# A hybrid decoder trunk (gated linear recurrence beside stick-breaking attention): one f32 copy of the mixer's output, and one split per engine and level of the recurrence

## The chip, the cores and the metric

The kernel runs on one core of a Trainium2 chip. The metric is the device time of one execution in microseconds (us). A core has five engines that work from their own instruction queues: PE (TensorE, matrix multiplies), DVE (VectorE), ACT (ScalarE), POOL (GpSimd) and SP, which here issues nearly all DMAs. An instruction starts when all ahead of it in its own queue have started and what it waits for in the others is done.

## The reference

One layer, 2048 rows, width 1024. The normalised rows are projected to 4096 columns; four heads A (a gated linear recurrence, 128 wide) and eight heads B (stick-breaking attention, 64 wide) each give 512 columns; both go through a normalisation and a gate, then one output projection. A per-layer embedding is projected, normalised, gated and added; a last normalisation ends it.

```
u = rmsnorm(h, norm_g);  proj = u @ w_in
k_a = (1 - lb) * sigmoid(-a_f);  f = 1 - k_a;  q_a = silu(a_q)
S_t = diag(f_t) S_{t-1} + k_t v_t^T;   o_t = S_t^T q_t              # group A
A[t,s] = sigmoid(z_ts) * prod_{s<j<t} (1 - sigmoid(z_tj)), s < t    # group B
y = concat(headnorm(o_a) * silu(a_g), headnorm(o_b) * silu(b_g))
h = h + y @ w_out
pe = rmsnorm(p @ w_ple_proj);  gate = sigmoid(rmsnorm(h) @ w_ple_gate)
out = rmsnorm(h + gate * pe)
```

## The kernel before, in words

Every large product is made from float16 parts: a float32 operand is stored as a high and a low half (`split`, L75: an ACT copy that rounds, L76, then a DVE instruction that takes the remainder, L77), and three matmuls (high·high, high·low, low·high) make one product.

The 2048 rows are four chunks of 512 (`CH`), done last chunk first. The columns are eight groups, B0, A0, B1, A1 to B3, A3; a group is one pair of B heads or one A head. The main loop (L829 to L843) goes over 8 groups x 4 chunks = 32 units. The projection of a unit (`proj_A` L407, `proj_B` L432) is the stream of PE work; while it runs, the rest of the earlier unit (`mix_A` L483, `mix_B` L596), the preparation of the rows (`prep_x`) and of the next group's weights are stepped in between. The kernel text gives this interleaving by a count of PE work; a scheduler then sets the final order in each engine's queue from its own times, so a change in one place can move instructions elsewhere.

`mix_A` is the recurrence over one chunk as a tree of seven levels. `kq` holds k (elements 0 to 511 of a row) and q (512 to 1023) in float32. At level lv, in blocks of B = 2^lv columns, the early half of each pair of blocks of q meets the late half of k: 12 small matmuls (`lps`, 64 columns) per level, 84 per unit and 1344 in all. `parts(lv)` (L499) splits 256 elements of q into the tiles `qch`, `qcl` (packed) and, from level 1, 256 elements of k into `kp0` or `kp1` by turns, in place; the other elements of those are zero (L490, a POOL memset of 1024 elements per unit) or come from the level before. k's first split (L492) and its last (L555) have 512 elements. `update(lv)` multiplies the rest of q and k by the decay (L514). L555's result is transposed by DMA for the state's update.

```
def parts(lv):
    B = 1 << lv
    qc[lv] = f16("qch", (P, CH // 2)), f16("qcl", (P, CH // 2))
    split(q3(qc[lv][0], B), q3(qc[lv][1], B), v4(q_, B)[:, :, 0, :], p2(SQF))
    if lv > 0:
        kh, kl = kp[(lv + 1) % 2]
        split(v4(kh, B)[:, :, 1, :], v4(kl, B)[:, :, 1, :], v4(k_, B)[:, :, 1, :], p2(SKB))
```

`y_out` (L374) ends every unit: it splits the unit's 512 x 128 result y (`ys`, 512 elements per partition) and stores both halves to the DRAM tensors `y_d`. The final stage (L853 to L872) goes over 16 blocks of 128 rows: `final_out` (output projection: 48 matmuls from `fy`, 12 of the embedding), `final_tr`, `final_gate` (48 matmuls). `fy` comes from DMA transposes out of `y_d`, one chunk at a time (L695, L701, L859).

The program begins with `prep_first` (L262): rows of x (`kq_t`, `gs_t`, `e_t`) are loaded and squared on ACT (L291), the first weights are split (L132 on ACT, L133 on DVE, both scaled by `gm`, which POOL multiplies once at L277), and x is turned on PE into `xt` and split into `xh`, `xl`. `prep_x` then loads the next rows into `raw_t` and squares them (L231).

Of the kernel before, what the change touches and what calls it, by code (L numbers as in the profile page):

```python
# [28 lines left out]
def p2(e):  # L29
    return float(2.0 ** e)  # L30
# [3 lines left out]
def trunk_kernel(  # L34
# [25 lines left out]
    BUFS = dict(jk=1, kq=2, fa=2, e0=2, e1=2, gs=3, qs0=2, qs1=2, kn=1, sc=2, y=2, kp0=1, kp1=1, qh=2, ql=2, qch=2, qcl=2,  # L60
                vh=2, vl=2,  ys=1, wt=2, at=2, raw=5)
# [4 lines left out]
    def f16(tag, shape=(P, CH)):  # L66
        return wk.tile(list(shape), F16, name=tag + "_t", tag=tag, bufs=BUFS[tag])
# [44 lines left out]
    y_d = [dt_(f"y{n}_d", [S, D]) for n in "hl"]  # L112
# [261 lines left out]
    def y_out(y, eg, c):  # L374

        ys = f16("ys", (P, 2, CB, P))
        split(ys[:, 0], ys[:, 1], y, p2(SY))
        for i in range(2):
            dst = y_d[i][c * CH : (c + 1) * CH, eg * P : (eg + 1) * P]
            if (eg, c) == (LAST, NC - 1):  # L380
                if i == 0:
                    y_fetch(c)
                nc.sync.dma_start(yt[c][i][:, eg, :].rearrange("p (b t) -> p b t", t=P), ys[:, i].rearrange("p b e -> p (b e)"), transpose=True)
            nc.sync.dma_start(dst.rearrange("(b p) e -> p b e", p=P), ys[:, i])
# [22 lines left out]
    def proj_A(u, g, h, c):  # L407
        w = ws[g]
        kq, f_ = f32("kq", (P, 2, CH)), f32("fa")
        k_, q_ = kq[:, 0, :], kq[:, 1, :]  # L410

        def use(i, ps):
            if i == 0:
                nc.scalar.activation(k_, ps, AF.Sigmoid, scale=-UN)
                nc.vector.tensor_scalar(k_, k_, oml[:, h : h + 1], None, op0=ALU.mult)
                nc.vector.tensor_scalar(f_, k_, -1.0, 1.0, op0=ALU.mult, op1=ALU.add)
            else:
                nc.scalar.activation(q_, ps, AF.Sigmoid, scale=UN)
                nc.vector.scalar_tensor_tensor(q_, ps, UN, q_, op0=ALU.mult, op1=ALU.mult)
# [61 lines left out]
    state = {}  # L481

    def mix_A(h, c, kq, f_, vh, vl, gs):  # L483
# [67 lines left out]
        split(qh, ql, q_, p2(SQF))  # L551
# [129 lines left out]
    def done(eg, c):

        if eg != LAST or c in yt:
            return
        y_tiles(c)

    def y_tiles(c):
        n = NC - 1 - c
        pool, tags = ((kv, ("bkv0", "bkv1")), (xpool, ("xh0", "xl0")))[n % 2]
        if n < 2:  # L690
            yt[c] = [pool.tile([P, KD, CH], F16, name="fy", tag=t) for t in tags]
        else:
            yt[c] = yt[c + 2]

    def y_fetch(c):  # L695

        y_tiles(c)
        for ks in (slice(0, LAST), slice(LAST + 1, KD)):
            for i in range(2):
                src = y_d[i][c * CH : (c + 1) * CH, ks.start * P : ks.stop * P]  # L700
                nc.sync.dma_start(yt[c][i][:, ks, :], src, transpose=True)  # L701
# [151 lines left out]
    for c in reversed(range(NC)):  # L853
        while c not in yt:
            if not step_tasks(99):
                clock[0] = min(t.ready for t in tasks)
        yh, yl = yt[c]
        for i in range(2 if c < NC - 1 else 0):
            nc.sync.dma_start(yt[c][i], y_d[i][c * CH : (c + 1) * CH, :], transpose=True)  # L859
# [33 lines left out]
    def full_rows(rs, gkv, gyt, cc, bb):  # L893
# [3 lines left out]
        for t, src in zip((yh, yl), y_d):  # L897
            nc.sync.dma_start(t[:, 0:4, :], src[rows, 0 : 4 * P], transpose=True)
# [108 lines left out]
```

## Time and profile before

| | |
|---|---|
| median of 3 runs | 1268.37 us (1267.89 to 1270.45) |
| the profiled execution | 1265.43 us, of which the span of its records 1263.4 us |
| busy: PE | 1212.4 us, 96% |
| busy: PE's weight loads | 775.6 us, 61% (beside the matmuls) |
| busy: DVE | 874.3 us, 69% |
| busy: ACT | 598.1 us, 47% |
| busy: POOL | 361.9 us, 29% |
| mean granted clock of PE | 0.988 |

A busy time is the time in which an engine worked on some instruction; matmuls overlap, so a matmul's own duration is longer than what it adds. A view of waits puts an engine's idle time down to the instruction that released it. Times in a timeline run from the start of the span.

### The profile page before, as it was taken

What the parts mean: (1) busy time and instruction counts of PE and PEld (TensorE: products, weight loads), DVE (VectorE), ACT (ScalarE), POOL (GpSimd) and SP (SyncE); (2) the same over time, 40 slices, a digit from 0 to 9 for tenths busy, and PEclk for the clock granted to TensorE, in tenths of its full rate; (3) what the DMA queues carried; (4) which work ended last, traced back from release to release, by engine and by line L of the source; (5) the groups of instructions that cost most, each with busy time, mean ns of one, the idle gap of its engine ahead of it and who ended that gap; (6) DMA issues with size and microseconds to landing.
All of it is one profiled execution on the core that took longest, in us unless ns stands there. A gap on an engine that the chain in (4) does not pass through costs nothing. (4 is left out here: it accounts for less than half of the span.)

```text
span 1263.4 us, 25838 instructions
## 1 busy us (share of the span) xinstructions
PE 1212.4 (96%) x9802; PEld 775.6 (61%) x9802; DVE 874.3 (69%) x1736; ACT 598.1 (47%) x1507; POOL 361.9 (29%) x472
## 2 busy tenths in 40 slices
PE   8887989999989999998999999998999999999997
PEld 7664767767756777676766776665544444444443
DVE  5679899976689996688998668999843334234233
ACT  7665645555554464463555445555532323223222
POOL 4246631114441112444111445101121211111112
PEclk9999999999999999999999999999999999999998
DMA  9877731246661046773125665744735327124111
GB/s 267 275 194 185 176 89 35 60 128 131 142 167 29 18 116 136 140 185 63 29 50 143 126 137 136 169 137 144 138 79 135 96 57 177 50 72 96 42 51 53
DMA packets 268964, 147.03 MB, mean 116 GB/s; under 512 B 213280, under 2 KB 237856, under 8 KB 268832
## 3 DMA queue, kind: packets, MB, share of 16 engines
q1 hardware_dynamic: 268688, 145.04, 46.7%
q8 instruction: 79, 1.29, 0.4%
q14 instruction: 53, 0.43, 0.1%
q10 hardware_dynamic: 144, 0.26, 0.1%
HBM read 52.44 MB, written 33.55 MB: 68 GB/s over the span
## 5 line engine op out<-in xcount | busy, mean ns | idle before, releaser
L160 PE MATMUL pj<-wh,xh 128*128 128x256 f16 x1024 | 282.3, 276 | 4.0 <-DVE ql_t L77 4.0
L160 PE MATMUL pj<-wl,xh 128*128 128x256 f16 x1024 | 282.5, 276 | 0.0
L160 PE MATMUL pj<-wh,xl 128*128 128x256 f16 x1024 | 282.4, 276 | 0.0
L160 PEld LDWEIGHTS <-xh 128*128 128x128 f16 x2048 | 201.5, 99 | 30.0 <-issue 0.8
L160 PE MATMUL pj<-xl,wh 128*128 128x512 f16 (+1 forms) x560 | 197.7, 363 | 5.1 <-DVE xl L260 3.6
L160 PE MATMUL pj<-xh,wh 128*128 128x512 f16 (+1 forms) x560 | 197.4, 363 | 3.3 <-ACT xh L76 2.4
L160 PE MATMUL pj<-xh,wl 128*128 128x512 f16 (+1 forms) x560 | 197.6, 362 | 0.0
L84 POOL TENSOR_TENSOR rs_y<-rs_v,mhalf 128x1 f32<-128x1 f32 (+2 forms) x87 | 77.5, 890 | 291.9 <-DVE rs_v L83 236.0
L160 PEld LDWEIGHTS <-at_t 128*128 128x128 f16 x1688 | 100.7, 99 | 91.8 <-issue 15.4
L160 PE MATMUL np<-wh,fy 128*128 128x512 f16 x512 | 156.0, 379 | 0.2 <-DVE gs_t L389 0.2
L160 PEld LDWEIGHTS <-wh 128*128 128x128 f16 x1120 | 101.1, 99 | 88.3 <-issue 6.2
L160 PEld LDWEIGHTS <-fy 128*128 128x128 f16 x768 | 74.2, 98 | 87.4 <-issue 0.3
L768 DVE TENSOR_TENSOR e_t<-e_t,kq_t 128x512 f32<-128x512 f32 (+2 forms) x33 | 22.3, 675 | 140.4 <-POOL kq_t L767 140.2
L160 PEld LDWEIGHTS <-xl 128*128 128x128 f16 x1024 | 101.4, 99 | 20.6 <-issue 4.1
L160 PE MATMUL np<-wh,at_t 128*128 128x512 f16 (+2 forms) x264 | 98.0, 373 | 0.0
L160 PE MATMUL np<-wl,at_t 128*128 128x512 f16 (+2 forms) x264 | 98.0, 373 | 0.0
L160 PE MATMUL np<-wh,wt_t 128*128 128x512 f16 (+2 forms) x264 | 97.9, 373 | 0.0
L624 DVE TENSOR_TENSOR_SCAN e_t<-e_t,reset 128x642 f32<-128x642 f32 x56 | 87.8, 1567 | 14.4 <-ACT e_t L619 14.1
L160 PE MATMUL np<-wl,fy 128*128 128x512 f16 x256 | 97.0, 379 | 0.0
L160 PEld LDWEIGHTS <-wl 128*128 128x128 f16 x560 | 54.0, 99 | 62.5 <-issue 7.5
L632 ACT CAST wt_t<-e_t 128x640 f16<-128x640 f32 (+1 forms) x64 | 44.8, 699 | 98.4 <-DVE e_t L629 73.8
L634 POOL TENSOR_TENSOR wt_t<-e_t,wt_t 128x512 f16<-128x512 f32 (+1 forms) x64 | 77.4, 1210 | 43.8 <-ACT wt_t L632 43.2
(193 smaller groups left out, 2279.6 us busy)
## 6 DMA issues: line engine op xcount, KB each, us to landing
raw_t<-w_in SPq DMA_DIRECT2D x61, 256.0 KB, 4.0
raw_t<-x_nat SPq DMA_DIRECT2D x56, 256.0 KB, 3.4
out<-y_t SPq DMA_DIRECT2D x31, 256.0 KB, 2.1
kq_t<-x_t SPq DMA_DIRECT2D x12, 512.0 KB, 4.7
bkv<-kn_t SPq DMA_DIRECT2D x64, 64.0 KB, 2.0
bkv<-ql_t SPq DMA_DIRECT2D x64, 64.0 KB, 2.0
bkv<-bkv SPq DMA_DIRECT2D x64, 64.0 KB, 2.3
gs_d<-gs_t SPq DMA_DIRECT2D x16, 256.0 KB, 3.3
```

The source lines that it names most:

```text
L84: nc.gpsimd.tensor_tensor(y, v, mhalf[:, 0:n], op=ALU.pow)
L160: nc.tensor.matmul(out_, lhsT, rhs, start=start, stop=stop)
L624: nc.vector.tensor_tensor_scan(fl(pr_), fl(f), fl(reset), 0.0, op0=ALU.mult, op1=ALU.max)
L632: nc.scalar.copy(wt[:, :, :w_], sg[:, :, :w_])
L634: nc.gpsimd.tensor_tensor(wt[:, :, 3 * P : 3 * P + lw], sg[:, :, :lw], wt[:, :, :lw], op=ALU.subtract)
L768: nc.vector.tensor_tensor(h_, h_, p_, op=ALU.add)
```

## The change

- `y_d` is one float32 tensor; `y_out` stores y as it is, without a split.
- A new `y_load(n)` reads one block of 128 rows of y (512 KB), splits it in two halves of 512 elements on ACT and DVE, and turns it with two DMA transposes. It is called for block 0 when the unit of the last group and chunk 3 is done, and for block n + 1 ahead of block n of the final stage.
- The tiles `kp0`, `kp1` hold high and low halves of k and q together (2048 elements), and are set to zero once, in the first `mix_A`, by two memsets that replace the sixteen.
- `parts(lv)` is one ACT copy and one DVE subtraction of 512 elements (of k and q together); the scales are put into k and q when they are made. k's first split falls away; its last goes into a tile of its own.
- The scores read q's early blocks where they lie: every second block of B elements, in place of packed columns.

```diff
-    y_d = [dt_(f"y{n}_d", [S, D]) for n in "hl"]
+    y_d = dt_("y_d", [S, D], F32)
...
     def y_out(y, eg, c):
 
-        ys = f16("ys", (P, 2, CB, P))
-        split(ys[:, 0], ys[:, 1], y, p2(SY))
-        for i in range(2):
...
-            nc.sync.dma_start(dst.rearrange("(b p) e -> p b e", p=P), ys[:, i])
+        dst = y_d[c * CH : (c + 1) * CH, eg * P : (eg + 1) * P]
+        nc.sync.dma_start(dst.rearrange("(b p) e -> p b e", p=P), y)
...
-                nc.vector.tensor_scalar(k_, k_, oml[:, h : h + 1], None, op0=ALU.mult)
-                nc.vector.tensor_scalar(f_, k_, -1.0, 1.0, op0=ALU.mult, op1=ALU.add)
+                nc.vector.tensor_scalar(k_, k_, oml[:, h : h + 1], p2(SKB), op0=ALU.mult, op1=ALU.mult)
+                nc.vector.tensor_scalar(f_, k_, -p2(-SKB), 1.0, op0=ALU.mult, op1=ALU.add)
...
-        kp2_ = [f16(f"kp{i}", (P, 2, CH)) for i in range(2)]
-        kp = [(t[:, 0, :], t[:, 1, :]) for t in kp2_]
-        nc.gpsimd.memset(kp2_[0], 0.0)
+        if not lvt:
+            for i in range(2):
+                lvt.append(f16(f"kp{i}", (P, 2, 2, CH)))
+                nc.gpsimd.memset(lvt[i], 0.0)
         nc.gpsimd.tensor_tensor(pr_, q_, k_, op=ALU.mult)
-        split(kp[1][0], kp[1][1], k_, p2(SKB))
...
+        def act(t, B):
+
+            return t[:, B : 2 * CH - B].rearrange("p (i m b) -> p i m b", i=2, b=B)[:, :, ::2, :]
 
         def parts(lv):
             B = 1 << lv
-            qc[lv] = f16("qch", (P, CH // 2)), f16("qcl", (P, CH // 2))
-            split(q3(qc[lv][0], B), q3(qc[lv][1], B), v4(q_, B)[:, :, 0, :], p2(SQF))
-            if lv > 0:
-                kh, kl = kp[(lv + 1) % 2]
-                split(v4(kh, B)[:, :, 1, :], v4(kl, B)[:, :, 1, :], v4(k_, B)[:, :, 1, :], p2(SKB))
+            hl = [lvt[lv % 2][:, i].rearrange("p i t -> p (i t)") for i in range(2)]
+            nc.scalar.copy(act(hl[0], B), act(kqf, B))
+            nc.vector.tensor_tensor(act(hl[1], B), act(kqf, B), act(hl[0], B), op=ALU.subtract)
...
-            kh, kl = kp[(lv + 1) % 2]
-            qch, qcl = qc.pop(lv)
+            kh, kl, qh, ql = (lvt[lv % 2][:, i, j, :] for j in range(2) for i in range(2))
+            early = lambda t, r_: t[:, r_].rearrange("p (n h b) -> p n h b", h=2, b=B)[:, :, 0, :]
...
-                mm3(lps[:, b, :], [(kh[:, r_], qch[:, s2]), (kh[:, r_], qcl[:, s2]), (kl[:, r_], qch[:, s2])])
+                mm3(lps[:, b, :], [(kh[:, r_], early(qh, r_)), (kh[:, r_], early(ql, r_)), (kl[:, r_], early(qh, r_))])
...
-        split(kp[0][0], kp[0][1], k_, p2(SKB))
+        kf = f16("wt", (P, 2, CH))
+        split(kf[:, 0], kf[:, 1], k_, 1.0)
...
+    def y_load(n):
+
+        c, b = NC - 1 - n // CB, CB - 1 - n % CB
+        rows = slice((c * CB + b) * P, (c * CB + b + 1) * P)
+        t = kv.tile([P, KD * CH], F16, name="yn", tag=f"bkv{n % 2}")
+        yf = t[:, 0 : 2 * D].bitcast(F32)
+        nc.sync.dma_start(yf, y_d[rows, :])
+        if n == 0:
+            yt["t"] = kv.tile([P, 4, KD, P], F16, name="fy", tag="bkv2")
+        yt[n] = [yt["t"][:, n % 2 * 2 + i] for i in range(2)]
+        hl = [t[:, (2 + i) * D : (3 + i) * D] for i in range(2)]
+        for hs in hss:
+            split(hl[0][:, hs], hl[1][:, hs], yf[:, hs], p2(SY))
+        for i in range(2):
+            nc.sync.dma_start(yt[n][i], hl[i], transpose=True)
...
+            n = (NC - 1 - c) * CB + CB - 1 - b
+            if n + 1 < NB:
+                y_load(n + 1)
+            yh, yl = yt[n]
```

The scheduler's order moves with it. The first place is POOL's queue at the start of the program; first before, then with the change (line numbers of the changed kernel are lower by 5 to 7 there).

```order
L331 MEMSET masks 128x448
L340 MEMSET reset 128x642
L490 MEMSET kp_t 128x1024
L337 AFFINE_SELECT masks<-masks 128x64 x7
L277 TENSOR_SCALAR gm<-gm 128x8
L338 AFFINE_SELECT masks<-masks 128x64
L84 TENSOR_TENSOR rs_y<-rs_v,mhalf 128x1
```

```order
L331 MEMSET masks 128x448
L340 MEMSET reset 128x642
L485 MEMSET kp_t 128x2048 x2
L337 AFFINE_SELECT masks<-masks 128x64 x7
L277 TENSOR_SCALAR gm<-gm 128x8
L84 TENSOR_TENSOR rs_y<-rs_v,mhalf 128x1
```

Two memsets of 2048 elements now stand where one of 1024 stood, ahead of the scaling of `gm`. The second place is ACT's queue at the same time, before and with the change: squares of x (L291), splits of the first weights (L132), the split of the turned x (L76).

```order
L291 ACTIVATE wt_t,ssx_164<-kq_t 128x512 x2
L132 ACTIVATE wh<-raw_t,gm 128x512 x4
L291 ACTIVATE wt_t,ssx_212<-gs_t 128x512 x2
L132 ACTIVATE wh<-raw_t,gm 128x512
L76 ACTIVATE xh<-xt 128x4x128
L132 ACTIVATE wh<-y_t,gm 128x512 x2
L76 ACTIVATE xh<-xt 128x4x128
L132 ACTIVATE wh<-sc_t,gm 128x512
```

```order
L291 ACTIVATE wt_t,ssx_163<-kq_t 128x512 x2
L291 ACTIVATE wt_t,ssx_211<-gs_t 128x512 x2
L132 ACTIVATE wh<-raw_t,gm 128x512 x5
L132 ACTIVATE wh<-y_t,gm 128x512 x2
L132 ACTIVATE wh<-sc_t,gm 128x512
L76 ACTIVATE xh<-xt 128x4x128
L291 ACTIVATE wt_t,ssx_238<-e_t 128x512
L76 ACTIVATE xh<-xt 128x4x128
```

The second pair of squares moved ahead of all weight splits, and the two splits of x behind them. The third place is DVE's queue in the last group A, at the first level of its third unit's recurrence, before and with the change (L499 and L507 are the changed kernel's lines of a level's split and update, `yn` is the tile of `y_load`).

```order
L77 SCALAR_TENSOR_TENSOR kp_t<-kq_t,kp_t 128x512
L415 TENSOR_SCALAR kq_t<-kq_t,oml 128x512
L77 SCALAR_TENSOR_TENSOR wt_t<-sc_t,wt_t 128x512
L419 SCALAR_TENSOR_TENSOR kq_t<-pj,kq_t 128x512
L514 TENSOR_TENSOR kq_t<-kq_t,fa_t 128x2x256
L416 TENSOR_SCALAR fa_t<-kq_t 128x512
L540 COPY_PREDICATED sc_t<-masks,lps 128x256
L77 SCALAR_TENSOR_TENSOR qs_t<-raw_t,qs_t 128x512
```

```order
L499 TENSOR_TENSOR kp_t<-kq_t,kp_t 128x2x256
L382 SCALAR_TENSOR_TENSOR gs_t<-pj,gs_t 128x256
L77 SCALAR_TENSOR_TENSOR wt_t<-sc_t,wt_t 128x512
L77 SCALAR_TENSOR_TENSOR wt_t<-kq_t,wt_t 128x512
L77 SCALAR_TENSOR_TENSOR yn<-yn 128x512
L507 TENSOR_TENSOR kq_t<-kq_t,fa_t 128x2x256
L77 SCALAR_TENSOR_TENSOR yn<-yn 128x512 x3
L133 SCALAR_TENSOR_TENSOR wl<-raw_t,gy,wh 128x512
```

Four splits of `yn` stand here with the recurrence's instructions; down to the last unit's last level there are 14 of them, 8 in the third unit and 6 in the fourth (seven blocks of y).

## Rows read from the trace of the kernel before

**Rows 1.** Busy time by stretch: us, PE, PEld, DVE, ACT, POOL (instructions), PEclk, DMA share, GB/s.

```profile
40.00:175.00 135.00, 119.90 (x977) 82.04 (x977) 113.84 (x156) 78.09 (x182) 72.59 (x82) 0.95 0.77 196
175.00:355.00 180.00, 180.00 (x1737) 128.70 (x1736) 146.19 (x301) 94.39 (x247) 50.04 (x69) 1.00 0.41 95
...
795.00:845.00 50.00, 46.82 (x458) 32.85 (x457) 47.55 (x110) 27.91 (x68) 7.98 (x7) 1.00 0.57 145
845.00:895.00 50.00, 45.65 (x398) 28.15 (x397) 44.39 (x101) 27.12 (x69) 6.32 (x6) 1.00 0.65 168
895.00:1250.00 355.00, 355.00 (x1742) 163.58 (x1740) 139.46 (x306) 112.17 (x288) 65.90 (x79) 1.00 0.34 83
```

**Rows 2.** PE's waits over the whole span: us in total, times, longest us.

```profile
PE op L160 <- DVE y_t L668: 14.5, 5, 3.9
...
PE pj L160 <- DVE xl L260: 3.6, 2, 2.3
```

**Rows 3.** PE's waits from 795 to 845 us.

```profile
PE lps L160 <- DVE qcl_t L77: 1.8, 2, 1.2
...
PE lps L160 <- ACT kp_t L76: 0.7, 2, 0.4
```

**Rows 4.** PE's waits from 845 to 895 us.

```profile
PE lps L160 <- ACT kp_t L76: 2.6, 3, 1.7
```

**Rows 5.** Splits by form: busy us, mean ns of one, then idle time before.

```profile
L77 DVE SCALAR_TENSOR_TENSOR qcl_t<-kq_t,qch_t 128x256 f16<-128x256 f32 x112 | 48.2, 431 | 3.8 <-ACT qch_t L76 3.6
...
L77 DVE SCALAR_TENSOR_TENSOR kp_t<-kq_t,kp_t 128x256 f16<-128x256 f32 x96 | 41.6, 434 | 6.3 <-ACT kp_t L76 6.3
...
L77 DVE SCALAR_TENSOR_TENSOR ys_t<-y_t,ys_t 128x512 f16<-128x512 f32 x32 | 25.0, 781 | 4.3 <-ACT ys_t L76 4.3
...
L77 DVE SCALAR_TENSOR_TENSOR kp_t<-kq_t,kp_t 128x512 f16<-128x512 f32 x32 | 21.8, 681 | 0.0
...
L76 ACT ACTIVATE kp_t<-kq_t 128x512 f16<-128x512 f32 x32 | 19.9, 622 | 0.0
...
L77 DVE SCALAR_TENSOR_TENSOR vl_t<-pj,vh_t 128x256 f16<-128x256 f32 x32 | 13.2, 415 | 3.3 <-ACT vh_t L76 3.3
```

**Rows 6.** Subtractions at L260, alone: duration ns min/median/max.

```profile
L260 DVE TENSOR_TENSOR xl<-y_t,xh x12: 659/678/1266, 41.6 to 114.2; 128x512 f16<-128x512 f32 x12
```

**Rows 7.** POOL's memsets by form: busy us, mean ns of one.

```profile
L611 POOL MEMSET wt_t<- 128x1280 f16 x8 | 9.3, 1162 | 12.8 <-DMA at_t<-wt_t 12.7
L490 POOL MEMSET kp_t<- 128x1024 f16 x16 | 15.2, 951 | 45.1 <-DMA at_t<-kp_t 39.0 <-DVE gs_t L389 6.2
```

**Rows 8.** Timeline of the start: start us, duration us, engine, line, operation.

```profile
5.90 0.24 POOL L277 TENSOR_SCALAR gm<-gm 128x8 f32<-128x8 f32 x1
8.08 2.07 ACT L132 ACTIVATE wh<-raw_t,gm 128x512 f16<-128x512 f32 x3 [1.13 <-DMA raw_t<-w_in]
...
11.34 0.19 ACT L291 ACTIVATION_READ_ACCUMULATOR wt_t<-gs_t 128x1 f32 x1
...
14.23 0.71 ACT L132 ACTIVATE wh<-sc_t,gm 128x512 f16<-128x512 f32 x1
...
15.56 0.74 DVE L133 SCALAR_TENSOR_TENSOR wl<-sc_t,gm,wh 128x512 f16<-128x512 f32 x1
```

**Rows 9.** Timeline around PE's gap at 36 to 40 us.

```profile
38.47 0.63 ACT L231 ACTIVATE raw_t<-raw_t 128x512 f32<-128x512 f32 x1 [0.47 <-DMA raw_t<-x_nat]
...
39.10 0.58 ACT L76 ACTIVATE qh_t<-pj 128x512 f16<-128x512 f32 x1
...
40.45 0.27 PE L160 MATMUL pj<-wh,xh 128*128 128x256 f16 x1 [3.97 <-DVE ql_t L77]
```

**Rows 10.** Small matmuls by form: busy us, mean ns of one.

```profile
L160 PE MATMUL lps<-qch_t,kp_t 128*128 128x64 f16 x896 | 64.8, 193 | 3.4 <-ACT kp_t L76 3.3
...
L160 PE MATMUL op<-vh_t,wt_t 128*128 128x128 f16 x128 | 21.5, 219 | 0.8 <-ACT jk_t L584 0.7
```

**Rows 11.** DMA issues: KB each, median us from issue to landing.

```profile
kq_t<-x_t SPq DMA_DIRECT2D x12, 512.0 KB, 4.7
```

More of the change, by code (lines that the diff above doesn't have):

```diff
@@ L58, in trunk_kernel @@
     ps_t = ctx.enter_context(tc.tile_pool(name="ps_t", bufs=1, space=PSUM))
-    BUFS = dict(jk=1, kq=2, fa=2, e0=2, e1=2, gs=3, qs0=2, qs1=2, kn=1, sc=2, y=2, kp0=1, kp1=1, qh=2, ql=2, qch=2, qcl=2,
-                vh=2, vl=2,  ys=1, wt=2, at=2, raw=5)
+    BUFS = dict(jk=1, kq=2, fa=2, e0=2, e1=2, gs=3, qs0=2, qs1=2, kn=1, sc=2, y=2, kp0=1, kp1=1, qh=2, ql=2,
+                vh=2, vl=2,  wt=2, at=2, raw=5)
     def f32(tag, shape=(P, CH)):
@@ L414, in use @@
                 nc.scalar.activation(k_, ps, AF.Sigmoid, scale=-UN)
-                nc.vector.tensor_scalar(k_, k_, oml[:, h : h + 1], None, op0=ALU.mult)
-                nc.vector.tensor_scalar(f_, k_, -1.0, 1.0, op0=ALU.mult, op1=ALU.add)
+                nc.vector.tensor_scalar(k_, k_, oml[:, h : h + 1], p2(SKB), op0=ALU.mult, op1=ALU.mult)
+                nc.vector.tensor_scalar(f_, k_, -p2(-SKB), 1.0, op0=ALU.mult, op1=ALU.add)
             else:
                 nc.scalar.activation(q_, ps, AF.Sigmoid, scale=UN)
-                nc.vector.scalar_tensor_tensor(q_, ps, UN, q_, op0=ALU.mult, op1=ALU.mult)
+                nc.vector.scalar_tensor_tensor(q_, ps, UN * p2(SQF), q_, op0=ALU.mult, op1=ALU.mult)
         yield from two_tiles(u, w, c, use)
@@ L481, in trunk_kernel @@
     state = {}
+    lvt = []
     def mix_A(h, c, kq, f_, vh, vl, gs):
@@ L511, in update @@
             T2 = T[lv].rearrange("p (n h) -> p n h", h=2)
-            act = kqf[:, B : 2 * CH - B].rearrange("p (i m b) -> p i m b", i=2, b=B)[:, :, ::2, :]
             other = T[lv].rearrange("p (n h) -> p h n", h=2).unsqueeze(3).broadcast_to([P, 2, nb, B])
-            nc.vector.tensor_tensor(act, act, other, op=ALU.mult)
+            nc.vector.tensor_tensor(act(kqf, B), act(kqf, B), other, op=ALU.mult)
             T[lv + 1] = wk.tile([P, nb], F32, name="Tn", tag=f"T{lv}")
@@ L520, in mix_A @@
         prh, prl = f16("qh"), f16("ql")
-        split(prh, prl, pr_, p2((SQF + 4)))
+        split(prh, prl, pr_, p2(4 - SKB))
         nc.gpsimd.memset(sc, 0.0)
@@ L530, in mix_A @@
                 r_ = slice(b * P, (b + 1) * P)
-                s2 = slice(b * 64, (b + 1) * 64)
-                mm3(lps[:, b, :], [(kh[:, r_], qch[:, s2]), (kh[:, r_], qcl[:, s2]), (kl[:, r_], qch[:, s2])])
+                mm3(lps[:, b, :], [(kh[:, r_], early(qh, r_)), (kh[:, r_], early(ql, r_)), (kl[:, r_], early(qh, r_))])
             if lv == 4:
@@ L550, in mix_A @@
         qh, ql = f16("qh"), f16("ql")
-        split(qh, ql, q_, p2(SQF))
+        split(qh, ql, q_, 1.0)
         scs = f16("wt", (P, 2, CB, P))
@@ L554, in mix_A @@
         split(sch, scl, sc, p2(SS - SQF - SKB))
-        split(kp[0][0], kp[0][1], k_, p2(SKB))
+        kf = f16("wt", (P, 2, CH))
+        split(kf[:, 0], kf[:, 1], k_, 1.0)
         ktt = f16("at", (P, 2, CB, P))
-        nc.sync.dma_start(ktt.rearrange("p l b d -> p (l b) d"), kp2_[0].rearrange("p l t -> p (l t)"), transpose=True)
+        nc.sync.dma_start(ktt.rearrange("p l b d -> p (l b) d"), kf.rearrange("p l t -> p (l t)"), transpose=True)
         kth, ktl = ktt[:, 0], ktt[:, 1]
@@ L675, in mix_B, with done @@
             yield 6.0
-    fin = {}
+    def done(eg, c):
+        if (eg, c) == (LAST, NC - 1):
+            y_load(0)
     yt = {}
[L681 to L701, printed above, removed]
+    def y_load(n):
[12 more added lines that the diff above has]
+            nc.sync.dma_start(yt[n][i], hl[i], transpose=True)
     def nat_proj(pool, tag, lh, ll, nk, w, res, cuts=((0, CH),)):
@@ L853, in trunk_kernel @@
     for c in reversed(range(NC)):
[L854 to L859, printed above, removed]
         pp = p_parts(lambda k: p_t[c, :, k, :], CH)
@@ L864, in trunk_kernel @@
             st = {}
-            run(final_out(st, lambda k: yh[:, k, sl], lambda k: yl[:, k, sl],
+            n = (NC - 1 - c) * CB + CB - 1 - b
+            if n + 1 < NB:
+                y_load(n + 1)
+            yh, yl = yt[n]
+            run(final_out(st, lambda k: yh[:, k, :], lambda k: yl[:, k, :],
                           lambda k: pp[k][0][:, sl], lambda k: pp[k][1][:, sl], rows), -1)
@@ L896, in full_rows @@
         yh, yl = gyt[:, :, 0:P], gyt[:, :, P : 2 * P]
-        for t, src in zip((yh, yl), y_d):
-            nc.sync.dma_start(t[:, 0:4, :], src[rows, 0 : 4 * P], transpose=True)
+        ya = f32("sc")
+        nc.sync.dma_start(ya, y_d[rows, 0 : 4 * P])
+        yp = [f16(f"kp{i}") for i in range(2)]
+        split(yp[0], yp[1], ya, p2(SY))
+        for t, p_ in zip((yh, yl), yp):
+            nc.sync.dma_start(t[:, 0:4, :], p_, transpose=True)
         nc.vector.memset(rs, 0.0)
```

7 lines of the change are left out of this document (removed).

## The prediction

> **What bounds the kernel now.** I began with the busy time by stretch [rows 1]. From 175 to 355 us PE is busy all 180.00 us, and in the final stage, from 895 to 1250, all 355.00: there nothing that ACT, DVE or POOL save can move the end, for PE is the stream that sets it. PE sits idle in a few places only. From 40 to 175 us it lacks 15.1 us, while the second and third chunks of x are prepared beside the first attention units. From 795 to 845 it lacks 3.2 us and from 845 to 895 it lacks 4.4 us: that is the last group A, and DVE is busy there for 47.55 and 44.39 of 50 us. So a change to DVE's work counts in the last group, and hardly elsewhere.
>
> Next came PE's waits. Over the whole span [rows 2] the largest is the output of the attention units waiting for y_t (14.5 us in 5 waits): the step from a group B to a group A, which hangs on POOL's and DVE's normalisation of that unit; the split of y comes after that instruction, not before it. Another 3.6 us are the split of x at L260. In the last group [rows 3, 4] PE waits for the recurrence: for q's low part (1.8 us) and k's high part (0.7 us) in the first half, and for k's high part (2.6 us) in the second. These 5.1 us are what the faster levels could win there.
>
> Last I read the start [rows 8] and PE's gap at 36 to 40 us [rows 9], because the order of ACT's queue changes there.
>
> **What the change costs, part by part.** The profiled execution, 1265.43 us, is the base; it lies 2.94 us below the median of 1268.37, and I add this back at the end.
>
> *The recurrence's levels.* Before, a unit's DVE splits are one of 512 elements and seven of q and six of k with 256 [rows 5]: 0.681 + 7 x 0.431 + 6 x 0.434 = 6.30 us. Afterwards they are seven of 512, now a subtraction rather than a scale-and-subtract. The nearest subtraction of that shape and those types is L260's [rows 6]: 0.678 us at the median, so 7 x 0.678 = 4.75 us, a gain of 1.55 us per unit. Its longest, 1.266 us, is an upper end for one that meets a busy POOL. ACT's seven copies take 7 x 0.622 us [rows 5]; ACT is busy for little over half of the last group [rows 1], so I don't count it. In the other twelve units PE has almost no gap to fill, and the gain there is 0.
>
> *The split of y.* It leaves every unit: 0.78 us of DVE [rows 5]. It counts at nothing in the middle, for the same reason. In the early stretch it could shorten PE's waits for L260 by one or two such splits; I take 0 and keep -1.6 us for the range.
>
> *The last group, first half.* Two units lose 2 x (1.55 + 0.78) = 4.7 us of DVE work. That is more than the 2.5 us that PE waits there for splits [rows 3]; a wait can't become less than nothing, so the gain is at most 2.5 us, and I take **-2.5 us** (ends 0 and -3.2, all of the idle time).
>
> *The last group, second half.* Two more units lose 4.7 us of DVE work. But the order shown above puts 14 splits of the new `yn` among the last two units' recurrences: at 0.68 to 0.78 us [rows 5] they add 9.5 to 10.9 us. The net is +4.8 to +6.2 us, against 50 - 44.39 = 5.6 us in which DVE was idle [rows 1]. At the upper price it overflows by 0.6 us, and the present waits of PE stay as they are: **+0.6 us**. The lower end is -2.6 us, the wait for k's part gone [rows 4]; the upper end is all of it before PE, +6.2 us.
>
> *The start.* On POOL two memsets of 2048 elements replace one of 1024. From the two sizes in the trace [rows 7], 256 elements more cost 1.162 - 0.951 = 0.211 us, so one of 2048 takes an estimated 1.80 us, two take 3.59, and the scaling of `gm` moves from 5.90 us [rows 8] to 8.54. That alone would cost little. But the order made of it puts both squares of the second block of rows ahead of all weight splits on ACT, and these squares wait for a load: they end at 11.34 + 0.19 = 11.53 us [rows 8]. Then come eight weight splits at 2.07 / 3 = 0.69 us, to 17.05, and behind them two splits of x at 0.62 (18.3), whose low halves on DVE (0.68) are ready at about 19.0. Before, the last operand of the first pass is ready at 15.56 + 0.74 = 16.30. PE's steady stream thus begins 2.7 us later. PE has a gap at 36 to 40 us that could swallow this, but it ends with an eviction on the same ACT queue [rows 9], behind squares that wait for loads into buffers which the same splits must free; the new order puts one more square ahead of it. I take **+2.8 us**, with 0 (the gap swallows it all) and +3.6 (one more square of 0.63 us and its read-out) as ends.
>
> *The scores.* They read q in place, with gaps between blocks. No row shows a matmul with such a moving operand. The nearest rows are of DVE: it takes 0.431 us for 256 elements of q read with gaps and 0.415 for 256 read packed [rows 5], so gaps cost 4% at most. I take 0. If a gapped operand ran at half speed, a score matmul would cost what 64 more columns cost in the small matmuls [rows 10], 0.219 - 0.193 = 0.026 us: 192 matmuls of the first level make +5.0 us, all 1344 make +35 us.
>
> [...]
>
> *The final stage.* Each block gains a load of 512 KB, two splits and two transposes. The load takes 4.7 us by the nearest DMA of that size [rows 11], the splits under 3; a block lasts 355 / 16 = 22.2 us, so they end within the block before if the transposes take less than 14 us. DVE is busy 139 of 355 us there and has room for 32 x 0.78 = 25 us. Term 0. The transposes out of DRAM that it replaces were hidden as well.
>
> The removed memsets on POOL save nothing, as nothing waits for them in PE's list.
>
> **Sum:** -2.5 + 0.6 + 2.8 = +0.9 us on 1265.43, which is 1266.3; with the 2.94 us between this execution and the median, **1269.3 us**.
>
> **The rivals.** A measurement of this kernel can tell about 0.2% (2.5 us) from no change.
>
> *Faster: the start is swallowed and the recurrence wins.* If PE's 4 us gap at 36 us ends when the loads say so, and not ACT's order, the start costs 0; if ACT and DVE, relieved of two instructions per level, also end the waits of the second half (-2.6) and shorten the early ones (-1.6), the sum is -2.5 - 2.6 - 1.6 = -6.7, or 1261.7 us. For it: all these waits are on ACT or DVE splits. Against it: the level's chain remains copy, subtraction, decay, with instructions of twice the length, and the 14 new splits.
>
> *Slower: the new splits of y stand in front of the recurrence.* DVE works in order. A split of `yn` waits for ACT's half and this for a load from DRAM; whatever of the recurrence stands behind it waits too, and so do PE's scores. It decides once DVE's added 9.5 to 10.9 us outgrow both the relief of 4.7 and the 5.6 us of idle time, or once one load is late. All of the net load before PE makes +6.2 rather than +0.6: -2.5 + 6.2 + 2.8 = +6.5, or 1274.9 us. For it: DVE at 89% of that stretch [rows 1]. Against it: at the same time PE has blocks of the final stage at hand to fill in.
>
> *Slower: gapped operands at reduced speed on PE*, +5 us for the first level alone: 1274.3 us; far worse if for all.
>
> *The levels gain nothing*, because an instruction of 512 elements costs as much as two of 256. The rows exclude it: 0.681 against 0.431 + 0.434 [rows 5].
>
> **How the numbers follow.** The forecast (the terms nearly cancel) has 0.36, with its own range from 1266 to 1272 (the small errors of its terms); the faster case, in whole or in half, 0.34; the splits of y in the way 0.23; gapped operands 0.07. So faster by over 0.2%: 0.34; within: 0.36; slower: 0.30. The range reaches from just beyond the faster case, 1260, to just beyond the slower ones, 1276, and leaves out the far end of the operands' case and of both others.
>
> **What would show it.** Right: PE's first steady matmuls about 2.8 us later, and its gap before 41 us ending as much later; the level's DVE instruction near 0.68 us; PE's waits for q's and k's parts from 795 to 845 us nearly gone; PE still without idle time in the final stage; the score matmuls at 193 ns. Wrong: a late start that has vanished by 45 us; waits of PE for the recurrence that grow in the last group, with `yn` ahead of them on DVE; a longer mean of the score matmuls; any wait in the final stage for the turned y.

## The result, and the profile after

The changed kernel takes 1278.47 us (median of 6 runs, 1276.62 to 1283.63) against 1269.41 us before (6 runs on the same chip): a ratio of 1.006 with a 95% interval of 1.0044 to 1.0077. It is slower by 0.6% (0.4 to 0.8%), some 8 us, and its time lies outside the range that was given.

The profile after is of an execution of 1283.63 us, the slowest of the six; x1 below gives a second one, of 1279.42 us. First the busy time by stretch of the changed kernel (columns as in [rows 1]).

```profile
0.00:40.00 40.00, 28.05 (x282) 26.51 (x283) 20.59 (x44) 24.36 (x61) 17.73 (x40) 0.87 0.85 244
40.00:175.00 135.00, 115.30 (x916) 79.37 (x914) 98.56 (x140) 75.32 (x176) 66.21 (x77) 0.94 0.77 198
...
795.00:845.00 50.00, 44.69 (x440) 30.81 (x438) 45.08 (x87) 25.59 (x52) 7.19 (x7) 0.97 0.41 123
845.00:895.00 50.00, 44.63 (x385) 28.94 (x384) 44.73 (x99) 27.38 (x63) 3.92 (x4) 0.97 0.60 181
895.00:1250.00 355.00, 349.88 (x1744) 162.14 (x1742) 157.16 (x327) 122.56 (x303) 63.02 (x75) 0.99 0.46 109
```

PE's idle time has grown to 19.7 us from 40 to 175 us and to 5.3 and 5.4 us in the two halves of the last group; from 895 us on 5.1 us are lacking where there was nothing before. DVE's busy time has fallen in the first half (47.55 to 45.08 us), and it did not help. PE's waits of the changed kernel, from 795 to 845, from 845 to 895 and from 895 to 960 us:

```profile
PE lps L160 <- ACT kp_t L498: 1.7, 1, 1.7
PE lps L160 <- DVE kp_t L499: 1.7, 1, 1.7
PE op L160 <- ACT jk_t L577: 1.4, 1, 1.4
...
PE lps L160 <- ACT kp_t L498: 4.9, 2, 3.6
PE sp L160 <- DMA at_t<-wt_t: 0.3, 1, 0.3
...
PE sp L160 <- DMA at_t<-wt_t: 3.5, 1, 3.5
PE lps L160 <- DVE kp_t L499: 1.4, 2, 0.9
```

The waits for the recurrence did not go, they grew (compare [rows 3, 4]), and a new one of 3.5 us stands at the state's update, for the transpose of k. The groups of instructions by form:

```profile
L499 DVE TENSOR_TENSOR kp_t<-kq_t,kp_t 128x512 f16<-128x512 f32 x112 | 79.3, 708 | 5.2 <-ACT kp_t L498 4.0
L498 ACT CAST kp_t<-kq_t 128x512 f16<-128x512 f32 x112 | 72.2, 644 | 91.1 <-PE lps L160 43.0 <-DVE kq_t L507 42.2 <-DVE kq_t L487 3.0
L160 PE MATMUL lps<-kp_t 128*128 128x64 f16 x1344 | 65.5, 193 | 10.0 <-ACT kp_t L498 6.9 <-DVE kp_t L499 3.1
L77 DVE SCALAR_TENSOR_TENSOR yn<-yn 128x512 f16<-128x512 f32 x32 | 21.8, 710 | 50.3 <-ACT yn L76 50.3
```

The single prices are near those forecast: 0.708 us for the level's subtraction, 0.644 for its copy, 0.710 for a split of y, 193 ns for a score matmul as before.

**Where the time goes.** To place the loss I add up the work of PE's matmuls in order (their columns, float32 ones four times; that weight is a choice, no run shows it: in the kernel before two `xt` matmuls start 112 ns apart at a granted clock of 1.00, and two float16 ones of 128 columns 56 ns, but with a weight of two the column of the changed kernel stays the same) and compare the times at which the same amount of work is reached. The table gives how many us later than in the profile of the kernel before a run is there. That profile is of an execution of 1265.43 us, 4 to 6 us under the medians of that kernel beside the runs below (1269 to 1272 us), so what tells is where a column grows, not its level. The profiles of the changed kernel, x5, x7 and x8 are of their slowest executions and that of x13 is of its fastest, so times are compared by the medians.

| at (us, before) | changed | x1, again | x2, y alone | x4 | x6 | x7 | x9 | x10 | x13 | x12 |
|---|---|---|---|---|---|---|---|---|---|---|
| 45.0 | 2.7 | 2.4 | 0.2 | -0.1 | -1.1 | 0.6 | 0.9 | 3.1 | -3.5 | -0.6 |
| 75.7 | 9.1 | 8.6 | 1.8 | 11.1 | 1.7 | 4.9 | 1.7 | 6.1 | -1.5 | 2.8 |
| 152.0 | 11.7 | 6.7 | 0.4 | 8.9 | 1.0 | 6.0 | 1.6 | 9.1 | -2.4 | 2.6 |
| 218.8 | 10.8 | 5.7 | 1.7 | 10.6 | 4.2 | 6.4 | 2.8 | 8.8 | -1.2 | 4.3 |
| 550.9 | 11.3 | 6.1 | 2.4 | 9.5 | 4.6 | 6.9 | 6.6 | 11.9 | -0.5 | 4.9 |
| 766.4 | 8.6 | 5.7 | -0.1 | 6.9 | 2.0 | 4.3 | 6.8 | 13.1 | -3.0 | 2.2 |
| 795.0 | 5.1 | 2.2 | -3.0 | 3.9 | -1.5 | 1.8 | 7.0 | 11.4 | -6.0 | -0.2 |
| 904.1 | 11.3 | 7.4 | -0.1 | 10.2 | 5.1 | 5.6 | 6.9 | 14.6 | -2.0 | 2.0 |
| 950.2 | 18.7 | 14.4 | 2.3 | 17.2 | 12.3 | 7.6 | 6.9 | 14.6 | 4.2 | 2.6 |

After 950 us no column moves any more. The changed kernel loses at two places: in the first 150 us, and from 795 to 950 us, by 13.6 us (12.2 in x1). Between them, at the step from group B to A from 766 to 795 us, it gains 3.5 us in both profiles. Below, "the last group loses" counts from 766 to 950 us with that gain in it, which makes 10.1 us here (8.7 in x1).

How much of a growth is chance can be read from runs whose queues have the same order. From 170 us on x10 has the order of the kernel before on PE, DVE, ACT and POOL, and yet it loses 3.2 us from 795 to 950 us: that much in one column says nothing. The four profiles with the changed kernel's order there (changed, x1, x4, x6) lose 12.2 to 13.8 us.

**The start.** The timeline of the changed kernel, first POOL, then ACT, DVE and PE:

```profile
2.64 3.55 POOL L485 MEMSET kp_t<- 128x2048 f16 x2
...
10.21 0.63 ACT L291 ACTIVATE wt_t<-gs_t 128x512 f16<-128x512 f32 x1 [4.85 <-DMA gs_t<-x_nat]
...
11.48 3.16 ACT L132 ACTIVATE wh<-raw_t,gm 128x512 f16<-128x512 f32 x5
...
11.87 0.28 DVE L296 TENSOR_SCALAR dg<-ident,rs_y 128x128 f32<-128x128 f32 x1
...
17.79 1.28 DVE L77 SCALAR_TENSOR_TENSOR xl<-xt,xh 128x512 f16<-128x512 f32 x2
...
12.20 3.54 PE L300 MATMUL xt<-dg,kq_t 128*128 128x128 f32 x16 [5.76 <-DVE dg L296]
15.87 1.16 PE L300 MATMUL xt<-dg,gs_t 128*128 128x128 f32 x8
```

The two memsets take 3.55 us (3.59 forecast), the squares hold ACT until 11.48, and the low half of x is ready at 19.07 (19.0 forecast). At 45 us the lag is 2.7 us (2.8 forecast), but that is luck. One thing was not in the forecast: the factor `dg` of the first block stands on DVE behind the second block's sums, and PE has nothing for 5.76 us. At 36 us the lag is 7.5 us (7.7 in x1), and PE's gap at 36 to 40 us, which by the forecast would end as much later, takes 3.2 us of it back: of its 3.97 us [rows 9] 0.8 are left (a row of PE's waits from 40 to 175 us):

```profile
PE pj L160 <- DVE ql_t L77: 0.8, 1, 0.8
```

And the lag does not stay at 2.7 us: at 76 us it is 9.

### The profile page after: what moved, and what is told of

Read it like the earlier page. It is cut to its first block, busy times and chain, and to the rows that moved or that the text cites. A ratio compares the mean times of both kernels' runs of the same rounds, so it can differ in the third digit from the quotient of the medians.

```text
span 1281.9 us, 25542 instructions
## 1 busy us (share of the span) xinstructions
PE 1219.2 (95%) x9802; PEld 779.1 (61%) x9802; DVE 860.5 (67%) x1624; ACT 584.4 (46%) x1395; POOL 344.9 (27%) x458
## 4 chain that ended last, share of the span: by engine, by line
PE 72%; DVE 9%; DMA 9%; ACT 4%; issue 3%; SPq 2%; POOL 1%; POOLq 0%; DVEq 0%; ACTq 0%
PE pj L160 37%; PE np L160 26%; PE op L160 3%; PE lps L160 2%; DVE wl L133 2%; PE z L160 2%; DMA at_t<-wt_t 1%; DMA raw_t<-w_out 1%; DMA yn<-y_d 1%; DVE e_t L617 1%; ACT wh L132 1%; DMA kq_t<-x_t 1%; DMA raw_t<-x_nat 1%; DMA raw_t<-w_gate 1%; DMA fy<-yn 1%
## 5 line engine op out<-in xcount | busy, mean ns | idle before, releaser
L498 ACT CAST kp_t<-kq_t 128x512 f16<-128x512 f32 x112 | 72.2, 644 | 91.1 <-PE lps L160 43.0
```

Of the source, the lines that this page charges most:

```text
L498: nc.scalar.copy(act(hl[0], B), act(kqf, B))
```

## The experiments

**x1, the changed kernel again**, for a second profile.

> The changed kernel again, for a second profile. In the first one its n-th piece of PE's work lies 2.7 us later than in the kernel before at 45 us, 10.8 us later from 190 us on, 5.1 us at 786 us, 18.7 us from 950 us on; its own time was 1283.63 us, 5 us over its median. Theory A (the order of the queues costs the time, once at the start and once in the last group): the same steps again within 2 us, the early one of 9 to 12 us above all. Theory B (the losses are chance of the loads): another pattern.

1279.42 us. The two steps are there again, the late one within 1.4 us. The early lag is 2.4 and 8.6 us at first, as in the first profile, but 5.7 rather than 10.8 at 219 us: the first group varies by some 5 us from run to run. Both theories hold in part, A for the places, B for the early size.

**x2, y alone**: the diff's hunks on `y_d`, `y_out`, `done`, `y_load` and the final stage; `mix_A`, `proj_A` and the sixteen memsets as before.

> The y part alone: y in float32, y_load and the final stage as changed, the recurrence as before (with its sixteen memsets). Theory A: no late start, so no lag to 780 us, then 5 to 10 us lost in the last group, where the splits of yn stand among the recurrence: 1273 to 1279 us. Rival (the y part is harmless, the longer level instructions delay the recurrence): 1268 to 1271 us.

1269.09 us, a ratio of 0.999 (0.9975 to 1.0004). The rival's time. The splits of `yn` stand in the last group here too (14 of them ahead of the last unit's y), and it loses 2.4 us there: 5.3 us from 795 us on, after a gain of 2.9 at the step before. So the 9.5 to 10.9 us more of DVE work are not by themselves what makes the changed kernel's 12.2 to 13.8 us, though they may not be free: the gains at two steps from group B to A (2.5 us near 575 us, 2.9 near 780) make up for what is lost here.

**x3, the levels alone.**

```diff
-        ys = f16("ys", (P, 2, CB, P))
+        ys = f16("wt", (P, 2, CB, P))
...
-        kp2_ = [f16(f"kp{i}", (P, 2, CH)) for i in range(2)]
+                lvt.append(f16(f"kp{i}", (P, 2, 2, CH)))
+                nc.gpsimd.tensor_scalar(lvt[i].rearrange("p l i t -> p (l i t)"), oml[:, 0:1].broadcast_to([P, 4 * CH]), 0.0, None, op0=ALU.mult)
```

> The levels' part alone: y split and stored as before (its tile shares the tag of another), and the two zeroings taken from the start of the program by making them depend on a value that is ready at 23 us. Theory A: nothing lost at the start, and the steps from a group B to a group A shorter, as in the changed kernel (2.7 and 3.5 us at two of them): 1261 to 1267 us. Rival (the longer level instructions cost the time): 1273 to 1279 us.

1321.65 us, 1.0405 (1.0378 to 1.0433), far past both. It is no measure of the levels. y's split took the tag `wt`, whose two buffers then serve it beside the splits of the scores and of k and the attention's weights; in this run PE's lag grows from 11.3 us at 219 us to 37.2 at 786, through groups in which no other run loses more than 4.2 us. That the shared buffers are the reason was argued, not tried.

**x4, zeroing later.**

```diff
-                nc.gpsimd.memset(lvt[i], 0.0)
+                nc.gpsimd.tensor_scalar(lvt[i].rearrange("p l i t -> p (l i t)"), oml[:, 0:1].broadcast_to([P, 4 * CH]), 0.0, None, op0=ALU.mult)
```

> The changed kernel with its two zeroings made to depend on a value that is ready at 23 us, so that POOL scales gm early again and the squares of the second block stand behind four weight splits as before. Theory A: the lag of 10.8 us at 190 us goes to 0 to 2 us, the loss in the last group stays: 8 to 11 us faster than the changed kernel, 1267 to 1271 us. Rival (the early lag comes from elsewhere: the order of the loads in the first group B, the strided operands): as the changed kernel, 1276 to 1280 us.

1281.43 us, 1.0091 (1.0064 to 1.0117): the rival's result. ACT's weight splits are early again and the lag at 45 us is gone, yet it is 11.1 us at 76. With no memset at all there POOL is free earlier than in the kernel before, and the scheduler made a third order: PE still waits 3.3 us for `dg` (a row of PE's waits of x4), and for x later on. The zeroing that replaces the memsets also holds POOL for 10.71 us, from 21.83 us on; how much of the lag is the order and how much this was not tried. So to keep the order, POOL's queue had to be kept as it was, which is x6.

```profile
PE xt L300 <- DVE dg L296: 3.3, 1, 3.3
PE pj L160 <- DVE xl L77: 3.0, 1, 3.0
```

**x5, yn later.**

```diff
-        t = kv.tile([P, KD * CH], F16, name="yn", tag=f"bkv{n % 2}")
+        pool, tag = (kv, f"bkv{n}") if n < 2 else (xpool, ("xh0", "xl0")[n % 2])
+        t = pool.tile([P, KD * CH], F16, name="yn", tag=tag)
```

> The changed kernel, but from the third block on yn lies in the buffers of the first chunk's x, which come free with the last projection, so that the loads and splits of blocks 2 and 3 can't stand among the last two recurrences. In the second profile of the changed kernel ACT waits 5.5 us at 866 us for a load of yn, with the recurrence's copy behind it. Theory A (that wait, and not the length of the level's instructions, makes the loss in the last group): 4 to 7 us faster than the changed kernel, 1272 to 1275 us. Rival (DVE's load as a whole makes it): no more than 2 us faster, 1276 to 1279 us.

1273.1 us, 1.0015 (0.9998 to 1.0031), as theory A has it by its time, which is 0.4 to 0.5% under the changed kernel's. In the profile, that of the slowest of the twelve executions, the last group loses 7.3 us (from 4.4 at 766 to 11.7 at 950), against 8.7 and 10.1. By the time the early loads and splits of `yn` explain over half of the loss, by the profile the smaller part; which is nearer stays open. What they do can be read in x1, on ACT's timeline and then PE's:

```profile
871.98 1.15 ACT L76 ACTIVATE yn<-yn 128x512 f16<-128x512 f32 x2 [5.52 <-DMA yn<-y_d]
873.03 0.61 ACT L76 ACTIVATE qs_t<-raw_t 128x512 f16<-128x512 f32 x1
873.55 0.60 ACT L498 CAST kp_t<-kq_t 128x512 f16<-128x512 f32 x1
...
874.21 0.23 PE L160 MATMUL lps<-kp_t 128*128 128x64 f16 x1 [3.61 <-ACT kp_t L498]
```

ACT waits 5.52 us for a load of y; the recurrence's copy stands behind it, and PE behind that.

**x6, the start kept.** One memset of 1024 elements as before, the rest of the zeroing after the first group's attention:

```diff
-                nc.gpsimd.memset(lvt[i], 0.0)
+                lf = lvt[i].rearrange("p l i t -> p (l i t)")
+                h = 2 * CH if i == 0 else 0
+                if i == 0:
+                    nc.gpsimd.memset(lf[:, 0:h], 0.0)
+                nc.gpsimd.tensor_scalar(lf[:, h:], flag[:, 0:1].broadcast_to([P, 4 * CH - h]), 0.0, None, op0=ALU.mult)
```

> The changed kernel with one memset of 1024 elements at the start, as before, and the rest of the zeroing made to depend on a value that is ready after the first group's attention. All queues then have the order of the kernel before up to about 117 us. Theory A (the early lag of 6 to 11 us is the order of the queues): lag at 190 us within 2 us of the kernel before; 5 to 9 us faster than the changed kernel, 1270 to 1274 us. Rival (it is something that the levels or the float32 store bring, whatever the order): 1277 to 1280 us.

1277.19 us, 1.0042 (1.0026 to 1.0058). The lag at 152 us is 1.0 us, as theory A says: with ACT, DVE and PE in the order of the kernel before up to 117 us the early lag does not arise. But 3.2 us come back by 219 us (in that stretch the new zeroing holds POOL for 3.32 + 5.37 us; that it is the reason is only argued), and the gain in time is 0.18%, some 2 us, not 5 to 9. The loss in the last group is untouched (10.3 us).

**x7, k first.**

```diff
+        kf = f16("wt", (P, 2, CH))
+        split(kf[:, 0], kf[:, 1], k_, 1.0)
         qh, ql = f16("qh"), f16("ql")
         split(qh, ql, q_, 1.0)
...
-        kf = f16("wt", (P, 2, CH))
-        split(kf[:, 0], kf[:, 1], k_, 1.0)
```

> The changed kernel with k's last split written ahead of the scores' split. The second profile shows PE waiting 3.6 us at 931 us for k's transpose, whose split stands behind that of the scores on ACT. Theory A: this wait goes; 0 to 4 us faster than the changed kernel, 1275 to 1279 us. Rival (the wait is for the transpose's DMA, whatever the split's place): the same, 1278 to 1280 us.

1270.65 us, 0.9992 (0.9977 to 1.0007): 0.7% less than the changed kernel, more than either theory gave it. The last group loses 3.3 us rather than 8.7 to 10.1. Here is what stood in the way, in x1 on ACT, SP and PE:

```profile
924.81 1.15 ACT L76 ACTIVATE yn<-yn 128x512 f16<-128x512 f32 x2 [1.34 <-DMA yn<-y_d]
925.87 0.61 ACT L76 ACTIVATE wt_t<-sc_t 128x512 f16<-128x512 f32 x1
926.39 0.57 ACT L712 ACTIVATE kp_t<-np 128x512 f16<-128x512 f32 x1
...
926.96 0.61 ACT L76 ACTIVATE wt_t<-kq_t 128x512 f16<-128x512 f32 x1
...
928.33 1.24 SPq L550 DMA_TRANSPOSE at_t<-wt_t  x1
...
931.57 0.29 PE L160 MATMUL sp<-vh_t,at_t 128*128 128x128 f16 x1 [3.62 <-DMA at_t<-wt_t]
```

k is final once the last level's update is done, but its split (`wt_t<-kq_t`) stands on ACT behind the scores' split (`wt_t<-sc_t`), which needs the last scores, and behind the splits of `yn`. The transpose starts late, and PE waits for it. Before, the scheduler had put this split (in the tile `kp0`) ahead: in the last unit it started at 907.4 us, before the last scores at 909.3. PE's waits from 790 to 960 us, of x1 and then of x7:

```profile
PE lps L160 <- ACT kp_t L498: 6.7, 4, 3.6
PE sp L160 <- DMA at_t<-wt_t: 4.0, 2, 3.6
PE lps L160 <- DVE kp_t L499: 2.9, 3, 1.6
```

```profile
PE lps L160 <- ACT kp_t L498: 3.8, 4, 1.6
PE op L160 <- ACT jk_t L577: 3.3, 1, 3.3
PE lps L160 <- DVE kp_t L499: 1.9, 2, 1.7
```

The wait for the transpose is gone, and those for the recurrence are less by 3.9 us, for the queue behind it moves up as well; 2.0 us come back as a wait for a square. ACT still waits 4.27 us for a load of y in x7, but PE's longest wait for the copy behind it is 1.6 us: with k's work out of the way the queue stands that wait.

**x8, the three edits together** (x5, x6 and x7).

> The three edits together. Theory A (they mend separate losses): 1262 to 1268 us, a little under the kernel before, as the shorter steps from B to A remain. Rival (the order falls out anew each time and gives back what one edit won): 1269 to 1276 us.

1268.77 us, 0.9974 (0.9957 to 0.9992): under the kernel before, if not as far as hoped. The last group loses 3.2 us, as in x7.

**x9, k late in the kernel before.**

```diff
-        split(kp[0][0], kp[0][1], k_, p2(SKB))
+        kf = f16("wt", (P, 2, CH))
+        split(kf[:, 0], kf[:, 1], k_, p2(SKB))
```

> The kernel before, with one thing of the change: k's last split goes into a tile of its own, which puts it behind the scores' split in ACT's queue. Theory A (this place, and not the length of the level's instructions, makes most of the loss in the last group): 4 to 8 us slower than the kernel before, all of it after 795 us. Rival (it needs the changed levels and the splits of yn beside it): within 2 us of the kernel before.

1269.62 us, 0.9987 (0.9975 to 0.9999). Theory A falls in this form: the late place alone loses nothing (6.8 at 766 us, 6.9 at 950). What saves it is PE's queue. In the last unit, the last scores, the transpose of k on SP and the state's update:

```profile
913.67 0.19 PE L160 MATMUL lps<-qch_t,kp_t 128*128 128x64 f16 x1
...
917.13 1.24 SPq L558 DMA_TRANSPOSE at_t<-wt_t  x1
...
923.32 0.22 PE L160 MATMUL sp<-vh_t,at_t 128*128 128x128 f16 x1
```

The transpose lands at 920.35, 6.7 us after the last scores (3.4 us in the kernel before), but PE has 9.6 us of other matmuls in between and does not wait. In x1 it lands 9.1 us after them, and PE has 5.5 us of other matmuls.

**x10, a long memset in the kernel before.**

```diff
         nc.vector.tensor_scalar(reset[:, hd, 1 : P + 1], ident, p2(SA), None, op0=ALU.mult)
+    zz = kv.tile([P, KD * CH], F16, name="zz", tag="bkv0")
+    nc.gpsimd.memset(zz[:, 0 : 6 * CH], 0.0)
```

> The kernel before with a memset of 3072 elements more at the start, into a buffer not yet in use. The order of every queue is then that of the changed kernel up to about 117 us. Theory A (the early lag is the order that the memsets make): lag of 5 to 11 us at 190 us, as in the changed kernel, and 4 to 9 us slower than the kernel before at the end. Rival (the lag has another cause): within 2 us of the kernel before at 190 us.

1277.83 us, 1.0051 (1.0034 to 1.0069), with 8.8 us of lag at 219 us. One POOL instruction of 2.67 us, for which nobody waits, costs 6.5 us. It moves the scaling of `gm` to 8.51 us (5.90 before), and the order that the scheduler makes of it puts all weight splits on ACT behind the second block's squares, from 10.97 us on (the first at 6.22 before); up to 117 us ACT, DVE and PE have the order of the changed kernel. What the later `gm` costs by itself was not tried. The memset and PE's wait from 0 to 40 us:

```profile
2.63 2.67 POOL L344 MEMSET zz<- 128x3072 f16 x1
```

```profile
PE xt L300 <- DVE dg L296: 4.3, 1, 4.3
```

**x11, the start and k.** x6 and x7, with the late zeroing as plain memsets:

```diff
-                nc.gpsimd.tensor_scalar(lf[:, h:], flag[:, 0:1].broadcast_to([P, 4 * CH - h]), 0.0, None, op0=ALU.mult)
+                nc.vector.tensor_copy(lf[:, h : h + 1], flag[:, 0:1])
+                nc.gpsimd.memset(lf[:, h:], 0.0)
```

> The changed kernel with the start kept (one memset of 1024 elements there; the other two wait for a small DVE write that comes after the first group's attention, so POOL does plain memsets of some 2.7 us in place of 8.7) and k's last split ahead of the scores'. Theory A: lag at 190 us under 2 us, and no more than 3 us lost in the last group: 0.2 to 0.6% faster than the kernel before. Rival (the remaining lag of run x8 is not the zeroing): as x8, 0.997 of the kernel before at the least.

1268.47 us, 0.9982 (0.9968 to 0.9996). Faster than the kernel before, just short of what theory A gave. The lag is 3.0 us at 190 us, where theory A had under 2; 2.1 us are lost from 766 to 950 us.

**x12, the start, k and yn**: x11 with the edit of x5.

> As the run before it, and yn from the third block on in the late buffers as in x5. Theory A (the splits of yn do harm of their own): 1 to 3 us faster than the run before it. Rival (with k's split in its place they do no harm): the same within 1.5 us.

1266.71 us, 0.9967 (0.9951 to 0.9982), the fastest of all, 0.9% under the changed kernel. It is 0.15% under x11, as theory A has it, but the intervals overlap. The last group loses 0.4 us. Its stretches in the last group and after:

```profile
795.00:845.00 50.00, 45.62 (x451) 32.97 (x450) 46.38 (x97) 25.35 (x55) 7.19 (x6) 0.97 0.36 110
845.00:895.00 50.00, 46.25 (x370) 28.02 (x369) 45.21 (x94) 28.95 (x63) 3.71 (x4) 1.00 0.81 221
895.00:1250.00 355.00, 353.33 (x1763) 163.45 (x1762) 153.45 (x324) 124.22 (x308) 66.03 (x78) 1.00 0.44 105
```

**x13, y and k late**: x2 with the edit of x9.

> The y part as in x2, with the old levels, and k's last split behind the scores' as in x9; each of the two alone lost nothing. If k's late split and the splits of yn together make the loss in the last group (theory A): 4 to 8 us lost from 795 to 950 us beyond the 2.4 us of x2, 1274 to 1279 us. If it takes the new levels' instructions as well (rival): under 2 us beyond x2, 1268 to 1272 us.

1274.27 us, 1.0026 (1.0015 to 1.0036), against 0.999 for x2: 0.36%, 4.6 us. The last group loses 7.2 us, 4.8 beyond x2, and the two waits are there, with the old levels (PE's waits from 790 to 960 us):

```profile
PE lps L160 <- ACT kp_t L76: 5.5, 4, 2.6
PE sp L160 <- DMA at_t<-wt_t: 3.6, 1, 3.6
```

Here the transpose lands 8.2 us after the last scores, and PE has 4.6 us of other matmuls in between. So k's late split does harm where the splits of `yn` stand beside it, and needs no new level instructions for it; two things have changed against x9, the later landing and PE's shorter queue, and they were not tried apart.

## Why the prediction was wrong

**The step that failed** is the sum of the last group: "-2.5 us" for its first half and "+0.6 us" for its second. Measured, PE loses 13.6 us (12.2 in x1) more than before from 795 to 950 us. Three things are behind it.

- *k's last split had no term.* The change moves it from `kp0` to a tile of its own, and I read that as a renaming, though the third order shown ahead of the prediction has it, on DVE: `wt_t<-kq_t` behind `wt_t<-sc_t`. It moved the split behind the scores' split on ACT, and the transpose behind it. Putting it back (x7) wins 0.7%; from x6 to x8 and x11, which keep the start, the step is 0.6 to 0.7%, though x8 also moves `yn` and x11 has a cheaper zeroing. That is about the whole of the measured loss, but not a price of its own: x5, which leaves k's split where it is, wins 0.4 to 0.5%, so the two overlap. x9 and x13 show it too: nothing without the splits of `yn`, 4.6 us with them. With the split put back (x7, x11) 4.7 to 5.8 us are lost from 795 to 950 us, as in x2 (5.3) with the old levels.
- *The rival "the new splits of y stand in front of the recurrence" came true, on another engine.* I priced it by DVE's work against DVE's idle time; x2, with the same splits of y on DVE, is no slower than before. What holds the recurrence is ACT's wait of 5.52 us for the load of y, with the late split of k in the same queue. I had named that wait, and gave the case 0.23.
- *The gain of 2.5 us in the first half did not come.* PE waits 3.4 us there for the level's copy and subtraction, 2.5 before. A level is still a chain of copy (0.644), subtraction (0.708) and update (0.700). From the start of its first copy to the end of its last subtraction a level takes 1.34 us at the least and 1.98 at the median of the last four units; with two splits half as long it took 1.21 and 1.87. The busy time that left DVE shortened no chain.

**The start** was right in its prices and wrong in its path. Memset, squares and splits came within 0.1 us; the lag at 45 us did so by luck, as the wait for `dg` and the gap that gave way were both not in the sum. And "it ends with an eviction on the same ACT queue" was the end of my reading: the preparation of the next chunks of x then runs in another order through the first group B, and the lag is 6 to 12 us by 150 us, beyond my upper end of 3.6. In the kernel before the memset that makes this order costs 6.5 us (x10). In the changed kernel keeping the start is worth less, 0.1 to 0.2% (x6 against the changed kernel, x11 against x7), some 2 us; why it is less there stays open.

**Right** were these terms. The final stage hides the loads, splits and transposes of y: PE has no loss after 950 us in any run. The y part alone comes to nothing measurable (x2), as the difference of a loss and a gain that the sum did not have. The splits of 512 elements don't cost what two of 256 cost (0.708 us against 0.431 + 0.434). And the scores on gapped operands stay at 193 ns; the starts of two neighbours are 29.0 ns apart before (the median, at every level) and 30, 30 and 31 ns at the first three levels now, which is under 1 us over their 576 matmuls.

Not in the sum at all was a gain at the steps from group B to A, which the prediction put at nothing because "the split of y comes after that instruction": near 575 us 2.5 us in x2, 2.8 and 0.5 in the two profiles of the changed kernel; near 780 us 2.9 in x2 and 3.5 in both. x9 and x10, which keep y's split, gain 1.7 us at most at either. So it comes with the y part; by which wait was not tried.

What the new levels alone are worth stays open, since x3 doesn't measure them; x11 and x12 against x2 put them at 0.1 to 0.2%, within the intervals.

## What to carry to other kernels

When a change gives an intermediate a tile of its own, ask where its instruction will stand in its engine's queue, and what is late behind it; a diff that looks like a renaming can be the dearest line. Price an instruction that waits for a load by what stands behind it on that engine, not by its busy time (in x1 two splits of `yn`, 1.15 us of work, came after a wait of 5.52). Where a scheduler orders the queues, compare the order at the start before and after, and undo order changes that the change didn't need: here that and one moved split turned 1.006 into 0.998, and later loads of `yn` into 0.997 (x12, whose interval overlaps that of x11). And a change that measures as nothing can be two terms: y alone loses in one place what it wins in another.

## What the runs showed that was not expected

At the start the granted clock was lower after PE's idle time. PE's rows by stretch in the changed kernel (busy time, PEclk, DMA share, GB/s):

```profile
4.00:8.00 4.00, 2.44 (x17) 1.00 0.76 250
8.00:12.00 4.00, 0.00 (x0) 0.56 1.02 377
12.00:16.00 4.00, 3.67 (x17) 0.58 1.06 360
```

After PE fell idle at about 6.4 us the granted clock is 0.56 and 0.58 from 8 to 16 us (0.50 from 9 to 15), and the 16 matmuls of `xt` that come at 12.20 take 3.54 us, where the 8 at 15.87 take 1.16 (2.3 for sixteen). So the work behind the wait of 5.76 us was slower as well. Before, the same stretch from 8 to 12 us has a granted clock of 1.00, with PE busy for 2.05 us, in which those 16 matmuls ran; there the clock falls later and for less, behind a wait of 2.44 us: 0.76 from 12 to 16 us and 0.81 from 16 to 20. That the idle time is the cause was not tried.
